# Memory rows, first cached keys and early columns issued singly on the weights' queue; cache consumed at two thirds of the rate; queries one unit sooner

## The chip, the cores and the metric

The kernel runs on one core of one Trainium2 chip. The metric is the device time of one execution in microseconds (us); the median over the runs is compared. The engines are TensorE (PE, with its weight loads shown as PEld), VectorE (DVE), ScalarE (ACT), GpSimd (POOL) and SyncE (SP). SP, ACT and POOL also issue DMAs, each in its own queue.

## The reference, cut to what matters

One decoder layer is computed for two groups at once: a prompt of 256 tokens and 8 single new tokens ("decode" columns). All data is float32.

```
x = LN1(a*x + 0.5*SwiGLU_1(x))
x = LN2(a*x + W_out[RWKV7(x), ConvModule(x)])
x = LN3(a*x + MemCrossAttn(x, mem))        # 4 heads of 512, 256 memory tokens
x = LN4(a*x + 0.5*SwiGLU_2(x))

q = h @ w_mq;  s = q . mk / sqrt(512);  o = softmax(s) . mv;  out = o @ w_mo
prompt: mk, mv = mem @ w_mk, mem @ w_mv          (also returned)
decode: mk, mv = cache_mem_k, cache_mem_v        (8 x 256 x 4 x 512 each)
```

The change touches the stretch from the output projection of the mixer (second line) to that of the cross attention (third line).

## The kernel before, in words

Activations lie transposed: 128 features by 264 columns (256 prompt tokens and 8 decode tokens), 16 such tiles for the 2048 features. Each float32 operand is split into a high and a low float32r part, and a product is three matmuls (`mm3`, L301: lines L303, L304, L305). One such **block** of three matmuls covers 128x128 weights. Weights arrive in chunks of 128x1024 (512 KB, eight blocks) from one long plan: `fetch` (L252) issues them on SP into 3 raw buffers, `prepare` (L270) splits them on ACT (L188) and DVE (L189) into 4 high and 4 low buffers, `chunk` (L292) hands one to `gemm` (L318). So a split of chunk i+3 is emitted when chunk i is taken, and it needs the buffer of chunk i-1, which is free only when TensorE is through with that chunk.

**The order of the work.** The program is written as one driven stream (the matmuls) with side streams. `drive` (L139) adds a planned cost to a planned time `t` after each step of the driven stream (`BLK` = 0.3375 for a block) and then lets every side run that is due; a side's `yield` says how much planned time must pass before its next step. `finish` (L144) runs a side to its end at once, without waiting for planned time. An instruction is placed in its engine's queue by this order, though the scheduler may bring a ready instruction ahead of one that still waits. `with self.behind()` (L174) orders an instruction behind the last weight DMA issued so far, and `issue_after(self.pulse[...])` orders it behind the latest weight split.

**Mixer output projection** (`mixer_out` L1274, `out_proj` L1204). Parts of 512 output columns use all four accumulators (PSUM); DVE adds each accumulator to the residual `y` (L1243). After the second part the function `after` closes the mixer's memory and calls `att_start` (L1373), which calls `mem_reload` (L1321): 16 DMAs on POOL's queue bring back the 16 memory rows (128 KB each), and each row is split by ACT (L1328) and DVE (L1329).

**Memory units** (`mem_kv` L1331). A unit is 256 columns of the prompt's keys or values, 32 blocks. Four units are done earlier, in the LN1 stage; their results are read back from the outputs (`kv_early` L1400: 4 DMAs of 256 KB on SP). `LN2_UNITS` = 3 units run while LN2 is applied (`ln_apply` L411 as a side with a pace of 1.46: three DVE and two ACT instructions for each of 16 rows). Then `finish(*b.sides)` empties what is left of it.

**Attention** (`attention` L1406). Four query GEMMs (one per head, 64 blocks each, planned 21.6), each evicted by ACT (L1419), then the other 9 units (planned 10.8 each). Sides: `att_prompt` (L1448) for the prompt, and `att_decode` (L1489) for the cache. The cache is 64 tiles of 512 KB in 5 buffers, loaded on POOL's queue (L1502): for heads 0 to 3, in the order k0 k1 v0 k2 v1 v2 k3 v3, eight tiles each. A key tile also needs a broadcast query row (`qb`, 256 KB, L1509) and costs two DVE instructions (L1542). A value tile costs ACT L1565, DVE L1566, ACT `vh` (L188), DVE `vl` (L189) and two matmuls (L1571, L1572). Eight key tiles are followed by `dec_softmax` (L1547), eight value tiles by `dec_out` (L1576), which writes the decode columns of the head's output. After each tile the side waits `KV_GAPS` of planned time: 3.0 for a key, 1.5 for a value.

**Attention output projection** (`att_out` L1589, parts in `att_plan` L1358): six parts of 256 output columns over heads 0 to 2 (three chunks each), then six parts over head 3 (one chunk each), then two parts over all heads. Before each block row of head j it asks that the decode side be through with head j:

```
def ready(k):
    while self.decoded < k // 4:
        self.dec.step(self.t)
```

If the side is not that far in planned time, its steps are emitted there and then, ahead of the matmul.

Of the kernel before, what the change touches and what calls it, by code (L numbers as in the profile page):

```python
# [8 lines left out]
F32 = mybir.dt.float32  # L9
F32R = mybir.dt.float32r  # L10
I32 = mybir.dt.int32
AF = mybir.ActivationFunctionType
ALU = mybir.AluOpType
# [5 lines left out]
KD = 16  # L19
TP = 256  # L20
# [33 lines left out]
class Builder:  # L54
# [1266 lines left out]
    def mem_reload(self):  # L1321

        self.mh, self.ml = self.rawtiles()
        for k in range(KD):
            hi, lo = self.mh[k][:, :TP], self.ml[k][:, :TP]
            raw = lo.bitcast(F32)
            self.nc.gpsimd.dma_start(raw, self.mkeep[:, k])
            self.nc.scalar.activation(hi, raw, AF.Copy)  # L1328
            self.nc.vector.tensor_tensor(lo, raw, hi.bitcast(F32), ALU.subtract)  # L1329

    def mem_kv(self, unit, dest):  # L1331

# [40 lines left out]
    def att_start(self, pool):  # L1373
        nc = self.nc
        self.mx = pool
        self.banks(1)
        self.mem_reload()
        eye = self.mt("eye", (128, TB, TB), F32R)
        z = self.mt("eye0", (128, TB * TB))
        nc.vector.memset(z, 0.0)  # L1380
        nc.vector.memset(z[:, 0 : TB * TB : TB + 1], 1.0)
        nc.scalar.activation(eye.rearrange("p a b -> p (a b)"), z, AF.Copy)
        self.eye = eye
        self.kvn = {}
        self.qs = {}
        self.oh = None
# [13 lines left out]
    def kv_early(self, units):  # L1400

        for u in units:
            o, cg, _ = u
            self.nc.sync.dma_start(self.kv_dest(u)(), self.kv_rows(o, cg))

    def attention(self, P, units):  # L1406
        nc = self.nc
# [81 lines left out]
    def att_decode(self):  # L1489

        order = [("k", 0), ("k", 1), ("v", 0), ("k", 2), ("v", 1), ("v", 2), ("k", 3), ("v", 3)]
        items = [(n, h, b) for n, h in order for b in range(TB)]
        keys = [(h, b) for n, h, b in items if n == "k"]
        nc, I = self.nc, self.I
        tiles, qb, pc = [], [], {}

        def load():
            while len(tiles) < len(items) and len(tiles) < self.used + KV_BUFS:
                n, h, b = items[len(tiles)]
                t = self.mt("kv", (128, 2, 512), bufs=KV_BUFS)  # L1500
                src = I["cache_mem_" + n][0, b, :, h].rearrange("(j s) d -> s j d", s=128)
                nc.gpsimd.dma_start(t, src)  # L1502
                tiles.append(t)

        def queries(n):
            while len(qb) < min(n, len(keys)) and keys[len(qb)][0] < len(self.scr):
                h, b = keys[len(qb)]
                t = self.mt("qb", (128, 512), bufs=3)
                nc.gpsimd.dma_start(t, self.scr[h][b : b + 1].to_broadcast([128, 512]))  # L1509
                qb.append(t)  # L1510

        self.used = nk = 0
        for n, h in order:
            while h >= len(self.scr):
                yield 0.6
            if n == "k":
                sc = self.mt("dsc", (128, 2, TB), bufs=2)
                for b in range(TB):
                    queries(nk + 2)
                    load()  # L1520

                    with self.tc.issue_after(self.pulse[1].ins):
                        self.dec_score(tiles[self.used], qb[nk], sc, b)
                    nk += 1
                    self.used += 1
                    yield KV_GAPS[0]
                pc[h] = yield from self.dec_softmax(sc)
            else:
                po = self.held.tile([128, 512], F32, tag="po", name=self.uid("po"))
                for b in range(TB):  # L1530
                    load()
                    with self.tc.issue_after(self.pulse[0].ins):
                        sums = self.dec_value(tiles[self.used], pc[h], po, b)
                    self.used += 1
                    yield KV_GAPS[1]
                    sums()
                yield from self.dec_out(h, po)
            self.decoded = h if n == "v" else self.decoded
# [167 lines left out]
WARM = 8  # L1706
FIRST = 0, 3, 3
LOAD = 7.8
KV_GAPS = 3.0, 1.5
OUT_PARTS = ((0, [0, 1, 2, 3, 8, 9, 10, 11]), (8, []), (12, [12, 13, 14, 15]))  # L1710
FLUSH = 3.5, 1.72
ATT_GAPS = 1.24, 2.0, 3.5, 0.6
VBUFS = 2
LN_PACE = 2.4, 1.46
LN1_UNITS, LN2_UNITS, KV_BUFS = 4, 3, 5


def chained(wait, gen):
    yield wait
    yield from gen  # L1720


def program(tc, I, O):
    with ExitStack() as es:
        b = Builder(tc, I, O, es)
        b.consts()
        b.mark = b.xkeep = b.stats = b.lastfn = b.table = None
        P1 = b.ffn_plan(I["ffn1_w1"][0], I["ffn1_w3"][0], I["ffn1_w2"][0])
        units = b.mem_plan()
        b.plan_add([[u[2]] for u in units[:LN1_UNITS]])  # L1730
        PX = b.mixer_plan()
        PA = b.att_plan(units[LN1_UNITS:])
        P2 = b.ffn_plan(I["ffn2_w1"][0], I["ffn2_w3"][0], I["ffn2_w2"][0])

        with tc.tile_pool(name="mem", bufs=1) as mpool:
            b.place(mpool, GAPS[0])
            with tc.tile_pool(name="ffn1", bufs=1) as pool:
                b.gate_places(pool, 0, GAPS[1])
                b.xs = b.load_x(mpool)

                def ffn1():
                    g = b.ffn(pool, P1)
                    n = 0
                    while True:
                        try:
                            c = next(g)
                        except StopIteration as e:
                            b.L = e.value
                            return
                        n += 1  # L1750
                        if n == 100:
                            b.lnv = b.loaded("lnv", [128, 8 * KD])
                            b.start(b.mixer_consts())
                        if n == 300:
                            b.start(b.mem_rows(mpool))
                        yield c

                b.drive(ffn1())
                b.start(b.ln_apply(b.L, "ln1", 4 * EPS), LN_PACE[0])
                for u in units[:LN1_UNITS]:  # L1760
                    b.drive(b.mem_kv(u, lambda: mpool.tile([128, 2, 256], F32, tag="mo", name=b.uid("mo"), bufs=1)))
                b.finish(*b.sides)
        mix = ExitStack()
        pool = mix.enter_context(tc.tile_pool(name="mix", bufs=1))
        y = b.ytiles()
        b.oa, b.cc = y[:8], y[8:]
        b.drive(b.mixer(pool, PX))

        att = ExitStack()

        def after():
            mix.close()
            b.raw = es.enter_context(tc.tile_pool(name="raw", bufs=1))
            for k in range(KD):
                b.place(b.raw, 128 if k else GAPS[2], (f"rh{k}", T + 2, F32R), (f"rl{k}", T + 2, F32R))
            b.att_start(att.enter_context(tc.tile_pool(name="att", bufs=1)))

        b.drive(b.mixer_out(PX, after))
        b.start(b.ln_apply(b.L, "ln2", EPS), LN_PACE[1])
        rest = units[LN1_UNITS:]  # L1780
        b.kv_early(units[:LN1_UNITS])
        for u in rest[:LN2_UNITS]:
            b.drive(b.mem_kv(u, b.kv_dest(u)))
        b.finish(*b.sides)
        b.drive(b.attention(PA, rest[LN2_UNITS:]))
        b.drive(b.att_out(PA))
        att.close()
        b.banks()
        with tc.tile_pool(name="ffn2", bufs=1) as pool:
            b.gate_places(pool, KD, GAPS[3])  # L1790

            def ffn2():
                b.L = yield from b.ffn(pool, P2, b.L)

            rows = b.start(chained(300.0, b.final_start(pool)))
            states = b.start(chained(80.0, b.rw_states(pool)))
            b.drive(ffn2())
            b.finish(states, rows)
            b.final(b.L, pool)


def build(tc, I, O):
    if MANUAL:
        with tc.manual_schedule():
            program(tc, I, O)
    else:
        program(tc, I, O)
# [66 lines left out]
```

## Time and profile before

| | us |
|---|---|
| median of 3 runs | 2519.65 |
| lowest, highest | 2515.61, 2521.88 |
| profiled execution, its own time | 2526.33 |
| its span in the profile | 2524.6 |
| busy PE, DVE, ACT, POOL | 2470.9, 1582.8, 1195.0, 261.7 |
| mean granted TensorE clock | 0.993 |

The page says what the engines did in 2524.6 us. Matmuls overlap in the pipeline, so a busy share of 98% does not say how fast TensorE went; the count of matmuls in a stretch and the granted clock do. All stretches below are in us from the span's start.

### The profile page before, as it was taken

How to read it: one execution, taken by the hardware profiler on the slowest of the kernel's cores; microseconds unless marked ns; L12 is line 12 of the kernel's file. 1: busy time of each engine (PE TensorE's matmuls, PEld its weight loads, DVE VectorE, ACT ScalarE, POOL GpSimd, SP SyncE). 2: the span in 40 equal slices, each digit the busy share in tenths (PEclk: the TensorE clock that was granted, in tenths of full speed). 3: DMA queues.
4: the chain of work that ended last, by engine and by line, in shares of the span. 5: the costliest groups of instructions: out<-in, count | busy, mean ns of one | idle time of the engine just before them, and what ended most of it. 6: DMA issues, size and time to landing. Idle time of an engine off the chain costs nothing. (4 is left out here: it accounts for less than half of the span.)

```text
span 2524.6 us, 53420 instructions
## 1 busy us (share of the span) xinstructions
PE 2470.9 (98%) x22328; PEld 2417.2 (96%) x22328; DVE 1582.8 (63%) x2545; ACT 1195.0 (47%) x1802; POOL 261.7 (10%) x422
## 2 busy tenths in 40 slices
PE   9999999999999999999989999999999999999998
PEld 9999999999999988988889888989999999999998
DVE  5545444444557599799777566789655545554465
ACT  5444433444446555455646354657444434444443
POOL 1300000000000001000110222220132500000000
PEclk9999999999999999999999999999999999999999
DMA  7656655555557754544476799976677755655554
GB/s 228 188 183 220 203 183 182 183 183 178 179 181 212 221 151 132 149 131 139 128 251 224 262 293 305 322 226 191 195 215 217 237 182 184 183 178 183 176 180 131
DMA packets 452211, 497.89 MB, mean 197 GB/s; under 512 B 22096, under 2 KB 418640, under 8 KB 451968
## 3 DMA queue, kind: packets, MB, share of 16 engines
q1 hardware_dynamic: 417840, 417.09, 54.0%
q0 software_dynamic: 20992, 67.22, 8.4%
q10 hardware_dynamic: 13136, 10.15, 1.2%
q8 instruction: 175, 2.87, 0.5%
q14 instruction: 68, 0.56, 0.1%
HBM read 477.76 MB, written 16.63 MB: 196 GB/s over the span
## 5 line engine op out<-in xcount | busy, mean ns | idle before, releaser
L189 DVE TENSOR_TENSOR wlo<-raw,whi 128x1024 fp32r<-128x1024 f32 (+1 forms) x791 | 961.4, 1216 | 850.6 <-ACT whi L188 847.3
L188 ACT ACTIVATE whi<-raw 128x1024 fp32r<-128x1024 f32 (+1 forms) x791 | 823.0, 1041 | 1035.6 <-PE acc L304 856.6
L303 PE MATMUL acc<-xh,whi 128*128 128x264 f32 x2864 | 828.7, 290 | 15.3 <-DVE y L1243 7.3
L304 PE MATMUL acc<-xl,whi 128*128 128x264 f32 x2864 | 820.2, 287 | 0.6 <-DVE xl L189 0.6
L305 PE MATMUL acc<-xh,wlo 128*128 128x264 f32 x2864 | 816.7, 286 | 0.5 <-DVE wlo L189 0.5
L303 PEld LDWEIGHTS acc<-xh,whi 128*128 128x128 f32 x2864 | 540.3, 189 | 23.8 <-ACT rh L1328 7.5
L304 PEld LDWEIGHTS acc<-xl,whi 128*128 128x128 f32 x2864 | 542.0, 189 | 3.7 <-DVE xl L189 0.8
L305 PEld LDWEIGHTS acc<-xh,wlo 128*128 128x128 f32 x2864 | 541.0, 189 | 2.3 <-DVE wlo L189 1.1
L303 PE MATMUL acc<-rh,whi 128*128 128x264 f32 (+2 forms) x1600 | 456.8, 285 | 0.2 <-ACT lnx L397 0.2
L305 PE MATMUL acc<-rh,wlo 128*128 128x264 f32 (+2 forms) x1600 | 454.5, 284 | 0.0
L304 PE MATMUL acc<-rl,whi 128*128 128x264 f32 (+2 forms) x1600 | 453.4, 283 | 0.0
L304 PE MATMUL acc<-gl,whi 128*128 128x264 f32 x1408 | 400.2, 284 | 0.0
L305 PE MATMUL acc<-gh,wlo 128*128 128x264 f32 x1408 | 400.1, 284 | 0.0
L303 PE MATMUL acc<-gh,whi 128*128 128x264 f32 x1408 | 399.5, 284 | 0.0
L303 PEld LDWEIGHTS acc<-rh,whi 128*128 128x128 f32 x1600 | 300.8, 188 | 2.2 <-ACT lnx L397 0.4
L304 PEld LDWEIGHTS acc<-rl,whi 128*128 128x128 f32 x1600 | 301.7, 189 | 1.2
L305 PEld LDWEIGHTS acc<-rh,wlo 128*128 128x128 f32 x1600 | 300.7, 188 | 0.2
L305 PEld LDWEIGHTS acc<-gh,wlo 128*128 128x128 f32 x1408 | 264.5, 188 | 0.1
L304 PEld LDWEIGHTS acc<-gl,whi 128*128 128x128 f32 x1408 | 264.5, 188 | 0.0
L303 PEld LDWEIGHTS acc<-gh,whi 128*128 128x128 f32 x1408 | 264.3, 188 | 0.1
L1176 DVE SCALAR_TENSOR_TENSOR y<-u,cw,y 128x256 f32<-128x256 f32 x240 | 111.1, 476 | 0.6
L397 ACT ACTIVATE lnx<-acc 128x264 f32<-128x264 f32 x84 | 32.4, 386 | 64.8 <-PE acc L305 64.8
(350 smaller groups left out, 2089.9 us busy)
## 6 DMA issues: line engine op xcount, KB each, us to landing
raw<-in_ffn_w SPq DMA_DIRECT2D x509, 512.0 KB, 3.6
raw<-in_w_in SPq DMA_DIRECT2D x86, 512.0 KB, 3.8
raw<-in_w_mk SPq DMA_DIRECT2D x32, 512.0 KB, 3.4
raw<-in_w_mv SPq DMA_DIRECT2D x32, 512.0 KB, 5.4
raw<-in_w_out SPq DMA_DIRECT2D x32, 512.0 KB, 5.1
kv<-in_cache_mem_k POOLq DMA_DIRECT2D x32, 512.0 KB, 6.2
raw<-in_w_mq SPq DMA_DIRECT2D x32, 512.0 KB, 5.2
kv<-in_cache_mem_v POOLq DMA_DIRECT2D x32, 512.0 KB, 6.1
```

Source lines behind the costliest of these rows:

```text
L188: a = self.nc.scalar.activation(hi, src, AF.Copy)
L189: return a, self.nc.vector.tensor_tensor(lo, src, hi.bitcast(F32), ALU.subtract)
L303: nc.tensor.matmul(out, wh, xh, start=start, stop=False)
L304: nc.tensor.matmul(out, wh, xl, start=False, stop=False)
L305: self.mark = nc.tensor.matmul(out, wl, xh, start=False, stop=stop)
L397: self.lastfn = self.nc.scalar.activation(*args, **kw)
L1176: V.scalar_tensor_tensor(c[:, :TP], u[:, i : i + TP], w(i), c[:, :TP], ALU.mult, ALU.add)
```

## The change

`mem_reload` becomes a side: its 16 DMAs move from POOL's queue to SP's, each behind the last weight DMA, one per step, with the split of a row four steps after its DMA (`MEM_AHEAD` 4, `MEM_PACE` 1.5). A new side `kv_ahead` loads the first five cache tiles on SP's queue in the same manner; it waits `KV_WAIT` = 24.0 of planned time first, then 4.5 after each tile. `kv_early` becomes a side with a gap of 4.5. `KV_GAPS` goes from 3.0, 1.5 to 5.0, 2.5. `LN2_UNITS` goes from 3 to 2, so that the queries come one unit sooner and ten units follow them.

```
     def mem_reload(self):
         self.mh, self.ml = self.rawtiles()
-        for k in range(KD):
-            hi, lo = self.mh[k][:, :TP], self.ml[k][:, :TP]
-            raw = lo.bitcast(F32)
-            self.nc.gpsimd.dma_start(raw, self.mkeep[:, k])
-            self.nc.scalar.activation(hi, raw, AF.Copy)
-            self.nc.vector.tensor_tensor(lo, raw, hi.bitcast(F32), ALU.subtract)
+        for k in range(KD + MEM_AHEAD):
+            if k < KD:
+                with self.behind():
+                    self.nc.sync.dma_start(self.ml[k][:, :TP].bitcast(F32), self.mkeep[:, k])
+            if k >= MEM_AHEAD:
+                hi, lo = self.mh[k - MEM_AHEAD][:, :TP], self.ml[k - MEM_AHEAD][:, :TP]
+                self.split_from(lo.bitcast(F32), hi, lo)
+            yield MEM_PACE
+
+    def kv_ahead(self):
+        yield KV_WAIT
+        for b in range(KV_BUFS):
+            t = self.mt("kv", (128, 2, 512), bufs=KV_BUFS)
+            src = self.I["cache_mem_k"][0, b, :, 0].rearrange("(j s) d -> s j d", s=128)
+            with self.behind():
+                self.nc.sync.dma_start(t, src)
+            self.kvtiles.append(t)
+            yield KV_PACE
...
-        self.mem_reload()
+        self.reload = self.start(self.mem_reload())
+        self.kvtiles = []
...
-            self.nc.sync.dma_start(self.kv_dest(u)(), self.kv_rows(o, cg))
+            with self.behind():
+                self.nc.sync.dma_start(self.kv_dest(u)(), self.kv_rows(o, cg))
+            yield KV_PACE
...
-        tiles, qb, pc = [], [], {}
+        tiles, qb, pc = self.kvtiles, [], {}
...
-KV_GAPS = 3.0, 1.5
+KV_GAPS = 5.0, 2.5
...
-LN1_UNITS, LN2_UNITS, KV_BUFS = 4, 3, 5
+LN1_UNITS, LN2_UNITS, KV_BUFS = 4, 2, 5
+MEM_AHEAD, MEM_PACE, KV_WAIT, KV_PACE = 4, 1.5, 24.0, 4.5
...
-        b.kv_early(units[:LN1_UNITS])
+        b.finish(b.reload)
+        for u in units[:LN1_UNITS]:
+            b.kv_dest(u)()
+        ahead = b.start(b.kv_ahead())
         for u in rest[:LN2_UNITS]:
             b.drive(b.mem_kv(u, b.kv_dest(u)))
-        b.finish(*b.sides)
+        b.finish(ahead, *b.sides)
+        b.start(b.kv_early(units[:LN1_UNITS]))
         b.drive(b.attention(PA, rest[LN2_UNITS:]))
```

## Rows read from the trace of the kernel before

**Rows 1.** The page's first part: busy time of the engines, share of the span, instructions.

```profile
PE 2470.9 (98%) x22328; PEld 2417.2 (96%) x22328; DVE 1582.8 (63%) x2545; ACT 1195.0 (47%) x1802; POOL 261.7 (10%) x422
```

**Rows 2.** Busy time of each engine in chosen stretches: the stretch, its length, busy us and instructions of PE, PEld, DVE, ACT and POOL, the granted clock, the DMA share, GB/s. The first row is undisturbed FFN work. The others are, in order: the reload in the mixer's output projection, the rest of that projection, the three units, the queries, the nine units, the attention's output projection.

```profile
400.00:600.00 200.00, 200.00 (x1650) 200.00 (x1649) 96.69 (x101) 82.44 (x101) 0.00 (x0) 1.00 0.59 182
1255.00:1300.00 45.00, 37.68 (x285) 37.08 (x284) 29.22 (x58) 21.57 (x37) 13.13 (x23) 0.92 0.75 251
1300.00:1332.00 32.00, 32.00 (x265) 31.97 (x265) 27.98 (x56) 15.93 (x26) 0.00 (x0) 1.00 0.56 182
1332.00:1367.00 35.00, 35.00 (x291) 34.70 (x290) 32.00 (x67) 25.32 (x47) 0.00 (x0) 1.00 0.72 226
1367.00:1473.00 106.00, 99.05 (x788) 97.29 (x786) 58.34 (x96) 43.56 (x61) 19.47 (x31) 0.97 0.81 267
1473.00:1626.00 153.00, 144.68 (x1062) 133.98 (x1063) 107.72 (x207) 88.90 (x176) 42.16 (x66) 0.99 0.92 301
1626.00:1736.00 110.00, 105.21 (x818) 102.09 (x818) 90.41 (x179) 57.85 (x93) 23.29 (x38) 0.98 0.77 240
```

**Rows 3.** What TensorE waited for in the stretch 1255 to 1736: us in total, times, longest.

```profile
PE acc L303 <- DVE y L1243: 7.3, 1, 7.3
PE acc L303 <- ACT y L1419: 6.7, 4, 5.2
PE mis L1557 <- DVE p L1446: 4.5, 3, 2.2
PE mis L1481 <- ACT y L1419: 3.7, 1, 3.7
PE po L1571 <- ACT vh L188: 2.3, 2, 1.2
PE mis L349 <- DVE lns L345: 1.9, 1, 1.9
```

**Rows 4.** The timeline at the reload, of ACT, DVE and PE: start, length, engine, line, operation, output and input, count, and the idle time before it with what ended it.

```profile
1269.36 1.32 ACT L1328 ACTIVATE rh<-rl 128x256 fp32r<-128x256 f32 x3 [0.74 <-DMA rl<-mem]
...
1274.60 1.04 ACT L188 ACTIVATE whi<-raw 128x1024 fp32r<-128x1024 f32 x1
...
1275.67 1.23 DVE L189 TENSOR_TENSOR wlo<-raw,whi 128x1024 fp32r<-128x1024 f32 x1 [3.07 <-ACT whi L188]
1276.82 1.44 DVE L1243 TENSOR_TENSOR y<-y,acc 128x264 f32<-128x264 f32 x4
...
1277.38 0.56 PE L303 MATMUL acc<-xh,whi 128*128 128x264 f32 x1 [7.32 <-DVE y L1243]
```

**Rows 5.** What ACT waited for among the queries (1367 to 1473).

```profile
ACT whi L188 <- DMA raw<-in_w_mq: 27.9, 11, 7.9
```

**Rows 6.** The same columns as rows 2, in slices of 20 us.

```profile
1260.00:1280.00 20.00, 12.68 (x95) 12.50 (x94) 13.54 (x28) 10.87 (x22) 13.13 (x23) 0.86 0.91 302
1280.00:1300.00 20.00, 20.00 (x161) 19.97 (x161) 13.50 (x27) 6.80 (x8) 0.00 (x0) 0.97 0.77 264
1400.00:1420.00 20.00, 15.02 (x124) 14.80 (x122) 9.74 (x21) 5.36 (x6) 5.08 (x8) 0.94 0.91 307
1420.00:1440.00 20.00, 19.73 (x146) 19.43 (x147) 13.58 (x24) 7.89 (x11) 5.10 (x8) 0.89 0.82 253
1620.00:1640.00 20.00, 20.00 (x156) 19.58 (x156) 13.53 (x44) 9.89 (x24) 5.11 (x8) 1.00 1.03 356
```

**Rows 7.** DMA issues from 1200 to 1720: transfer, queue, count, KB each, median us to landing.

```profile
kv<-in_cache_mem_k POOLq DMA_DIRECT2D x32, 512.0 KB, 6.2
raw<-in_w_mq SPq DMA_DIRECT2D x32, 512.0 KB, 5.2
...
qb<-scr POOLq DMA_DIRECT2D x32, 256.0 KB, 7.0
...
rl<-mem POOLq DMA_DIRECT2D x16, 128.0 KB, 5.5
```

**Rows 8.** The timeline at the start of the attention's output projection, of DVE (a key tile of head 3) and of PE (the first matmul of the projection).

```profile
1625.99 0.69 DVE L1542 CUSTOM_DVE_ANT_0 kv<-kv,qb 128x512 f32<-128x512 f32 x1
...
1626.31 0.28 PE L303 MATMUL acc<-xh,whi 128*128 128x264 f32 x1
```

**Rows 9.** The instructions on the cache tiles: engine, operation, count, duration in ns (least, median, most), first and last start in us; the last line is of their loads.

```profile
L1565 ACT ACTIVATE kv<-kv,pc x32: 705/709/725, 1487.9 to 1675.2; 128x512 f32<-128x512 f32 x32
L1566 DVE SCALAR_TENSOR_TENSOR kv<-kv,pc x32: 719/745/750, 1488.8 to 1678.2; 128x512 f32<-128x512 f32 x32
L188 ACT ACTIVATE vh<-kv x32: 611/630/634, 1489.6 to 1679.1; 128x512 fp32r<-128x512 f32 x32
L189 DVE TENSOR_TENSOR vl<-kv,vh x32: 672/693/694, 1490.2 to 1680.3; 128x512 fp32r<-128x512 f32 x32
...
DMA to landing us min/median/max: 4.2/6.2/10.3
```

**Rows 10.** The timeline of head 3's softmax and values, of DVE, PE, ACT and POOL: the last key tile, the softmax's first and last steps, the first scaled value tile, two loads, the last value tile, and `dec_out`.

```profile
1651.73 0.68 DVE L1542 CUSTOM_DVE_ANT_0 kv<-kv,qb 128x512 f32<-128x512 f32 x1
...
1655.30 0.41 DVE L1442 TENSOR_REDUCE mx<-mis 8x1 f32<-8x256 f32 x1
...
1662.27 0.28 PE L1557 MATMUL mis<-ident,p 8*128 8x8 f32 x2 [2.25 <-DVE p L1446]
...
1662.81 1.95 ACT L1565 ACTIVATE kv<-kv,pc 128x512 f32<-128x512 f32 x3
...
1666.57 1.57 POOL L1502 DMA_DIRECT2D kv<-in_cache_mem_v  x2 [13.14 <-DVE vl L189]
...
1680.34 0.68 DVE L189 TENSOR_TENSOR vl<-kv,vh 128x512 fp32r<-128x512 f32 x1
...
1682.15 0.41 PE L1584 MATMUL mis<-ident,r 8*128 8x8 f32 x4
```

**Rows 11.** The weight splits from 1200 to 1720: line, engine, operation, count, busy us, mean ns.

```profile
L189 DVE TENSOR_TENSOR wlo<-raw,whi 128x1024 fp32r<-128x1024 f32 x138 | 169.5, 1230 | 108.0 <-ACT whi L188 106.4 <-PE mis L1463 1.2
L188 ACT ACTIVATE whi<-raw 128x1024 fp32r<-128x1024 f32 x139 | 147.1, 1058 | 148.6 <-PE acc L304 63.3 <-DMA raw<-in_w_mq 29.8 <-DMA raw<-in_w_mo 17.9
```

**Rows 12.** The last DVE step of LN2's 16 rows: count, durations in ns, first and last start.

```profile
L424 DVE TENSOR_TENSOR xl<-lnx,xh x16: 422/426/435, 1343.1 to 1372.8; 128x264 fp32r<-128x264 f32 x16
```

## The prediction, made before the changed kernel was run

> **What bounds the kernel now.** I read the page's busy shares first, then the stretches, TensorE's waits, and the timelines. TensorE is busy 98% [rows 1], so the time is its work plus its stalls. Undisturbed, 1650 matmuls take 200 us, 0.121 us each [rows 2], a block of three 0.364 us. The change takes no matmul away; it can only move stalls. Those within its reach lie between 1255 and 1736: idle 45-37.68 = 7.3 us at the reload, 7.0 in the queries, 8.3 in the units, 4.8 in the output projection [rows 2], together 27.4. After an idle stretch the granted clock is under full: 0.92, 0.97, 0.99 and 0.98 in these four [rows 2], which is at most 3.6+3.2+1.5+2.2 = 10.5 us of lost work, less what falls into the idle time itself. So about 35 us is all that this change can win, 1.4%.
>
> **What it removes.** *The reload, 7.3 us.* The chain runs backwards from the matmul at 1277.38: it waits for accumulators that DVE empties at 1276.82, behind a weight split at 1275.67, which waits for ACT's half at 1274.60, which stands in ACT's queue behind the splits of memory rows, each waiting for its DMA [rows 4]. Not the bandwidth but the order of ACT's queue holds TensorE. In the changed kernel a row is split four steps after its DMA. A step of 1.5 falls on the planned grid of 0.675, so it takes 2.03 planned, and 2.03x0.364/0.3375 = 2.2 us; four are 8.7 us, above the 5.5 us that such a DMA needs to land [rows 7]. ACT doesn't block; the 20 steps (44 us) end before the projection does at 1332. What stays is the emptying of four accumulators, 1.44 us [rows 4], and some lateness. I take 7 us as gained with its clock loss, between 3 and 9.
>
> The Trainium skill ("DMA: Bandwidth & Descriptors", section "Issuing engines are not separate DMA queues") says that DMAs from several engines end on the same 16 DMA engines and that another issuer saves only issue time. By that the move from POOL's queue to SP's gives nothing by itself, and the sum below would be 7 us worse. No row shows these rows on SP's queue; I count on the delayed split, not on the queue.
>
> *Queries and units.* ACT waits 27.9 us for query weights [rows 5], and TensorE then for evictions that stand behind those splits in ACT's queue: 6.7 and 3.7 us [rows 3]. The weights are late because too much is asked: a chunk is 524 KB per 24 matmuls, 2.91 us, or 180 GB/s; a key tile with its query row is 786 KB [rows 7] per gap of 3.0, which the grid of 1.35 rounds to 4.05 planned or 4.37 us, another 180. The 360 GB/s stand against at most 356 in any slice [rows 6]. With 5.0 the grid gives 5.4 planned, 5.82 us, 135 GB/s, and 315 in all. That fits, so I take 8 us off the queries (idle and clock) and 6 off the units, where the eviction wait of 3.7 and 1.1 of the 6.7 lie; half of the softmax and value waits [rows 3] stay, as they come from the order in the engines. In the output projection 4 us go: the softmax wait of 2.2 moves into what follows, some clock loss goes. Gains: 7+8+6+4 = 25 us; bounds 34, nearly all that there is, and 12, about half of what I take.
>
> **What it adds.** *The decode side no longer fits.* I add up the planned times, rounded up to the grid (1.35 in the queries, 0.675 after). Both kernels start head 0's keys at 25.7 planned after the first query matmul. Before: a key 4.05, later 3.375, a value 2.025. The output projection starts at 183.6 planned, when head 3's fourth key tile is emitted; v2 ended at 173.5 (asked for at 189.0), v3 ends at 219.4 (asked for at 232.2). The trace agrees: that key tile runs at 1625.99, and the projection starts at 1626.31 [rows 8]. After: a key 5.4, a value 2.7, so 8 keys 43.2 and 8 values 21.6. k0 ends at 71.6, k1 116.8, v0 139.1, k2 184.3. The projection starts at 194.4 with four of v1's eight tiles still to come. At its fifth block row `ready` asks for v1, at the ninth for v2: **eleven value tiles are emitted in two bunches (v1's last three and v2's first, then the rest of v2), ahead of matmuls that need them.** The rest of the schedule shifts: k3's last tile comes at 237.6, head 3 is asked for at 243.0, and **softmax and all eight v3 tiles are emitted there at once.**
>
> *First catch-up.* A value tile takes 0.709+0.630 us of ACT and 0.745+0.693 = 1.44 of DVE, 2.78 in a chain [rows 9]; on an idle machine one comes every 1.44. From the projection's start: the split of the fourth chunk ahead waits until TensorE is through with the first chunk at 8x0.364 = 2.9, and takes 1.06+1.23 [rows 11]; the last three v1 tiles behind it end near 10.5. `dec_out` took 1682.15-1681.02 = 1.1 us to its transposes and then some 1.3 of small splits [rows 10]: 13. TensorE has only the first chunk, and one of the next part if the scheduler brings it forward: idle 7 to 10. The second chunk runs to 16; only then is a buffer free for the next split, behind which six v2 tiles stand: 1.06+1.23+6x1.44+1.34+2.4 = 14.7, to 30.6. One more chunk can be brought forward: idle 12 to 15. Together 19 to 25 us; if the scheduler finds more to bring forward, 14. I take 20.
>
> *Second catch-up.* The softmax took 1662.6-1652.4 = 10.2 us in the old order, amid other work [rows 10]; its own steps add up to about 3. Eight values: 8x1.44+1.34 = 12.9; three of them must first be loaded into buffers that come free 2.8 us after the start, with at least 4.2 us to land [rows 9], which adds 0.5 to 2.5. `dec_out` 2.4. Nothing else can run, since the next six chunks all need head 3. Sum 3+14.4+2.4 = 20 us; from below 17, from above what the old trace shows with TensorE running beside it, 1682.2-1655.3 = 27 [rows 10]. I take 20, nearest to the bare durations, because the weight splits stop when TensorE does.
>
> *Clock after three idle stretches.* The 7.3 us idle left 0.86 and 0.97 in two slices, the 5 us idle 0.94 and 0.89 [rows 6], some 2 us of work beyond the idle time. I add 5, between 3 and 8.
>
> *One unit fewer under LN2.* Its 16 rows end at 1372.8, after the queries began [rows 12]. With 21.6 planned instead of 32.4 before `finish`, some eight rows are emitted in one go: 8x3x0.426 = 10.2 us of DVE. The queries use a row per 1.46 us and find them ready, but the next weight splits stand behind. `kv_ahead` waits 24.0, more than these 21.6, so `finish` also issues its five tiles **together, not singly**: 2.6 MB ahead of the next weights, 7.4 us at 356 GB/s [rows 6]. Seven chunks (20 us) of lead cover most. I add 2, bounds 0 and 8. The `kv_early` DMAs, now in the first query, come before the first key tile: nothing.
>
> **Sum.** Added 20+20+5+2 = 47, removed 25: +22 us. Against the profiled execution's 2526.3 us that is 2548; its time is 6.7 above the median of 2519.65, so against the median I say **2541.5**. All bounds at once give 0 (added 14+17+3+0, removed 34) and +56 (added 25+27+8+8, removed 12).
>
> **Rivals.**
> 1. *The catch-ups are hidden: faster.* Place: the two `ready` calls. If the scheduler orders the forced steps so that they run beside matmuls, or DVE and ACT are through with them early, the gain stands alone: 25-2 = 23 us, 2497; with a part of the stalls up to 2512. It decides from the point where both catch-ups with their clock cost less than 15 us. For it: the old trace has v3's tiles running beside matmuls. Against: there they were emitted 12.8 planned us before they were needed; now at the moment. Chance 0.17.
> 2. *They cancel:* catch-ups of 30 instead of 45 in all, within 7.5 us of no change, 2520. Chance 0.14.
> 3. *The reload gains nothing*, because SP's queue now holds rows and weights in one line and weights come late instead: 22+7 = +29, 2548.5. This is the skill's rule above taken alone. For it: 302 GB/s already in 1260 to 1280 [rows 6]. Against: the wait is one of queue order. Chance 0.10.
> 4. *The forecast*, +8 to +42 otherwise: 0.59.
>
> **How the numbers follow.** About 0.3% (7.6 us) is what a measurement of this kernel can tell from no change. Slower is 0.59+0.10 = 0.69, same 0.14, faster 0.17. For 8 in 10 the range leaves out the faster end of the first rival and the joint upper bounds: 2506 to 2562.
>
> **What the changed profile would show.** Right: no wait of L303 on DVE L1243 over 3 us at the reload; TensorE never idle for more than 2 us at once in the queries; three new idle stretches of 5 to 20 us in the output projection, ended by splits of `dec_out` (L189 or L188 on the decode columns), each followed by a clock under 1; value tiles at intervals near 1.4 us in them. Wrong: if those stretches are missing or under 15 us together, the catch-up was mispriced; if waits for query weights remain near 28 us, the demand was not the cause.

## The result and the profile after

The changed kernel takes **2556.69 us** (median of 4 runs, 2555.01 to 2560.45), the kernel before 2518.9 on the same chip (4 runs): ratio **1.014, 95% interval 1.0125 to 1.0156**. That is +38 us; the forecast was +22 to 2541.5, with 2506 to 2562 as the range. Ratios here and below leave out slow executions; the only ones are two of the 12 of experiment 9, which took 4600.43 and 4810.04 us.

The profiled execution of the changed kernel took 2555.01 us with a span of 2553.3, so the two traces differ by 28.7 us of span. The other 9 us of the 38 lie outside them: the trace of before comes from an execution 7.4 us above its median, that of after from one 1.7 below. I explain the 28.7.

First the stretches of the changed kernel that answer to [rows 2] without its first row: the reload, the rest of that projection, the units (two now), the queries, the other ten units, the attention's output projection (stretch, length, busy us and instructions of PE, PEld, DVE, ACT, POOL, granted clock, DMA share, GB/s).

```profile
1245.00:1290.00 45.00, 44.05 (x380) 42.25 (x380) 27.69 (x51) 18.50 (x24) 1.06 (x2) 1.00 0.41 141
1290.00:1321.00 31.00, 31.00 (x257) 30.96 (x256) 30.51 (x64) 18.39 (x34) 0.00 (x0) 1.00 0.70 231
1321.00:1345.00 24.00, 24.00 (x200) 23.70 (x200) 23.38 (x52) 18.56 (x36) 0.00 (x0) 1.00 0.63 208
1345.00:1459.00 114.00, 100.85 (x782) 98.81 (x782) 61.87 (x102) 48.09 (x72) 15.55 (x25) 0.93 0.82 277
1459.00:1607.00 148.00, 147.85 (x1130) 141.59 (x1129) 95.52 (x183) 77.95 (x149) 32.22 (x52) 1.00 0.87 282
1607.00:1757.00 150.00, 123.81 (x845) 108.80 (x845) 112.43 (x216) 75.20 (x127) 37.64 (x57) 0.87 0.70 229
```

The idle time of TensorE at the reload (1.0 us against 7.3) and in the units (0.2 against 8.3) is gone. In the queries it doubled (13.2 against 7.0), and the output projection went from 110 us with 4.8 idle to 150 us with 26.2 idle at a clock of 0.87.

TensorE's longest waits from 1200 to 1800 say who ended these stretches (total us, times, longest), as in [rows 3]:

```profile
PE po L1587 <- ACT vh L188: 12.2, 6, 3.5
PE acc L303 <- ACT whi L188: 11.0, 2, 9.6
PE mis L1573 <- DVE p L1462: 6.7, 2, 6.5
PE acc L303 <- ACT y L1435: 3.4, 2, 3.0
```

L1573, L1587, L1588 and L1600 are L1557, L1571, L1572 and L1584 of before; L1435 is L1419. Value tiles and a softmax now hold TensorE, one weight split holds it for 9.6 us, and the wait on L1243 of the reload has fallen to 0.9 us, further down the list.

For an account in one unit I use **lost time**: for every two matmuls in succession, the interval between their starts less the median interval of that kind of matmul (line and shape) in the same trace, added up by stage. It holds idle time and slow clock together.

| us | before | after | difference |
|---|---|---|---|
| up to the reload | 71.3 | 67.6 | -3.7 |
| reload and rest of that projection | 9.5 | 2.1 | -7.4 |
| queries | 11.0 | 19.5 | +8.5 |
| units behind the queries | 11.3 | 0.6 | -10.7 |
| attention's output projection | 7.9 | 41.0 | +33.1 |
| FFN 2 | 0.4 | 1.8 | +1.4 |
| from the last matmul to the end | 6.4 | 12.5 | +6.1 |
| sum | 117.8 | 145.1 | +27.3 |

The sum is 1.4 us short of the 28.7; these are not placed. Each column is one execution. The change touches nothing ahead of the reload, and yet that row differs by 3.7 us, and it lies between 65 and 73 in the traces of all kernels here: a few us in a row that adds up many stages can be chance.

**The catch-ups.** The timeline of TensorE in the output projection (start, length, tile, idle time before it and what ended it); these rows are the ends of its idle stretches:

```profile
1618.05 0.39 PE L1587 MATMUL po<-vh,eye 128*8 128x512 f32 x1 [2.20 <-ACT vh L188]
...
1622.88 0.59 PE L1600 MATMUL mis<-ident,r 8*128 8x8 f32 x4 [0.68 <-ACT r L1595]
...
1641.59 0.40 PE L1587 MATMUL po<-vh,eye 128*8 128x512 f32 x1 [3.47 <-ACT vh L188]
...
1645.47 0.81 PE L303 MATMUL acc<-xh,whi 128*128 128x264 f32 x2 [0.27 <-ACT xh L188]
...
1695.50 0.38 PE L1573 MATMUL mis<-ident,p 8*128 8x8 f32 x2 [6.52 <-DVE p L1462]
1698.65 0.59 PE L1587 MATMUL po<-vh,eye 128*8 128x512 f32 x1 [2.77 <-ACT vh L188]
...
1712.20 0.81 PE L303 MATMUL acc<-xh,whi 128*128 128x264 f32 x2 [0.27 <-ACT xh L188]
```

And the clock in slices of 5 us around the third (the columns of [rows 2]):

```profile
1685.00:1690.00 5.00, 3.98 (x34) 3.67 (x32) 3.58 (x6) 1.43 (x3) 0.70 (x1) 1.00 0.92 298
1690.00:1695.00 5.00, 0.00 (x0) 0.00 (x0) 3.50 (x7) 2.40 (x4) 0.00 (x0) 0.85 0.88 288
1695.00:1700.00 5.00, 1.35 (x4) 0.47 (x5) 3.52 (x7) 4.05 (x8) 0.14 (x1) 0.50 0.36 120
...
1710.00:1715.00 5.00, 4.05 (x18) 3.30 (x17) 0.67 (x4) 1.30 (x5) 2.52 (x5) 0.50 0.15 55
1715.00:1720.00 5.00, 5.00 (x34) 5.00 (x34) 2.66 (x5) 2.39 (x5) 4.06 (x7) 0.76 0.46 153
1720.00:1725.00 5.00, 5.00 (x44) 5.00 (x43) 5.00 (x8) 2.41 (x5) 4.12 (x7) 1.00 0.70 206
```

From 1615.9 to 1624.9, 1636.5 to 1645.5 and 1688.8 to 1712.2 no block of the projection runs: 9.0+9.0+23.4 = 41.4 us. Only the small matmuls of the value tiles, the softmax and `dec_out` run there, those of a value tile each ended by a split (`vh` on ACT, `vl` on DVE); a busy PE in these slices is not a working projection. When TensorE comes back, the clock is at 0.50 (the lower level, 1.2 GHz): the slices at 0.50 and 0.76 hold 18 and 34 matmuls, the undisturbed one at 1.00 holds 44.

**The start of the queries.** ACT's timeline, and the one row of SP's that matters:

```profile
1356.10 1.23 ACT L422 ACTIVATE lnx<-y,lnv 128x264 f32<-128x264 f32 x2 [1.37 <-DMA kv<-in_cache_mem_k]
...
1359.34 0.61 ACT L422 ACTIVATE lnx<-y,lnv 128x264 f32<-128x264 f32 x1 [1.39 <-DMA keep<-lnx]
1360.99 0.61 ACT L422 ACTIVATE lnx<-y,lnv 128x264 f32<-128x264 f32 x1 [1.04 <-DMA keep<-lnx]
...
1362.13 2.94 ACT L188 ACTIVATE whi<-raw 128x1024 fp32r<-128x1024 f32 x3
```

```profile
1347.84 3.52 SPq L1340 DMA_DIRECT2D kv<-in_cache_mem_k  x5
```

Three weight splits stand in ACT's queue behind the LN2 rows that `finish` emits at once. Two of these rows wait for a `lnx` buffer, which comes free only when its `keep` write has landed (1.39 and 1.04 us), and all five key tiles (2.6 MB) have been issued at 1347.84 to 1351. TensorE waits 9.6 us for the first of the three splits.

**The end.** The closing DRAINs of POOL and of SP, before and then after (line, engine, operation, count: shortest/median/longest ns, first and last start):

```profile
L1870 POOLq DRAIN  x3: 51/99/5795, 2517.6 to 2524.3; - x3
L1870 SPq DRAIN  x3: 7/7/7, 2523.8 to 2524.1; - x3
```

```profile
L1891 POOLq DRAIN  x3: 51/99/12242, 2540.3 to 2553.0; - x3
L1891 SPq DRAIN  x3: 7/7/7, 2546.2 to 2552.8; - x3
```

POOL's long DRAIN took 5.8 us and takes 12.2. Before, it ended at 2517.6+5.8 = 2523.4, and SP came to its own first DRAIN at 2523.8: the two engines were level. After, it ends at 2552.5, 6.3 us behind SP, and all wait for it. From the last matmul to the end it is 12.5 us instead of 6.4: 6.1 us that no step of the forecast has.

### The profile page after: what moved, and what is told of

Read it like the earlier page. It is cut to its first block, busy times and chain, and to the rows that moved or that the text cites. A ratio compares the mean times of both kernels' runs of the same rounds, so it can differ in the third digit from the quotient of the medians.

```text
span 2553.3 us, 53445 instructions
## 1 busy us (share of the span) xinstructions
PE 2480.2 (97%) x22328; PEld 2420.0 (95%) x22328; DVE 1581.7 (62%) x2545; ACT 1197.4 (47%) x1802; POOL 251.7 (10%) x401
## 4 chain that ended last, share of the span: by engine, by line
PE 85%; DVE 5%; DMA 4%; issue 3%; ACT 2%; POOL 0%; SPq 0%; POOLq 0%; ACTq 0%; DVEq 0%
PE acc L303 27%; PE acc L304 27%; PE acc L305 27%; DVE wlo L189 2%; DMA raw<-in_ffn_w 1%; ACT whi L188 1%; DMA raw<-in_w_mq 1%; DMA kv<-in_cache_mem_v 1%; DVE y L1176 1%; PE mis L1473 1%; DMA raw<-in_w_mo 0%; PE mis L1488 0%; DVE G L890 0%; PE mis L850 0%; PE mis L843 0%
## 5 line engine op out<-in xcount | busy, mean ns | idle before, releaser
L303 PE MATMUL acc<-xh,whi 128*128 128x264 f32 x2864 | 829.9, 291 | 18.0 <-ACT whi L188 11.8
L303 PEld LDWEIGHTS acc<-xh,whi 128*128 128x128 f32 x2864 | 541.8, 190 | 26.1 <-ACT whi L188 12.6
L303 PE MATMUL acc<-rh,whi 128*128 128x264 f32 (+2 forms) x1600 | 455.1, 284 | 0.2 <-ACT lnx L397 0.2
L303 PE MATMUL acc<-gh,whi 128*128 128x264 f32 x1408 | 399.6, 284 | 0.1
L303 PEld LDWEIGHTS acc<-rh,whi 128*128 128x128 f32 x1600 | 301.1, 188 | 1.0 <-ACT lnx L397 0.4
L303 PEld LDWEIGHTS acc<-gh,whi 128*128 128x128 f32 x1408 | 264.3, 188 | 0.4 <-ACT lnx L397 0.3
```

The source lines that it names most:

```text
L303: nc.tensor.matmul(out, wh, xh, start=start, stop=False)
```

## The experiments

Ratios are to the kernel before on the same chip, with their 95% intervals.

**1. The changed kernel with the old gaps.**

```
-KV_GAPS = 5.0, 2.5
+KV_GAPS = 3.0, 1.5
```

> The changed kernel with the old gaps (3.0, 1.5). If the decode side that no longer fits is what costs, the idle stretches in the attention's output projection go (33 us of lost TensorE time there against 8 before), the units get back some 5 to 10 us of stalls, and the time is 2526 to 2535 us against 2557. If the queue of the rows or the start of the queries is the main cost, it stays above 2545.

Measured 2527.98 us, 1.0016 (1.0003 to 1.0028). The catch-ups are gone: 5.9 us lost in the output projection. What is left of the change is no gain either. What TensorE still waits for from 1200 to 1800 is led by the split at the start of the queries:

```profile
PE acc L303 <- ACT whi L188: 9.1, 2, 8.5
PE acc L303 <- ACT y L1435: 5.5, 3, 3.9
PE po L1587 <- ACT vh L188: 3.9, 2, 2.1
```

**2. The kernel before with the new gaps alone.**

```
-KV_GAPS = 3.0, 1.5
+KV_GAPS = 5.0, 2.5
```

> The kernel before with the new gaps (5.0, 2.5) alone: 27 steps are then forced in planned time, since the projection is asked for 10.8 earlier than in the changed kernel. If the forced steps are the cost: 33 to 45 us added in the output projection, 15 to 20 removed in queries and units, 2535 to 2548 us. If a slower rate costs nothing by itself: 2500 to 2512 us, as the DMA demand falls.

Measured 2554.57 us, 1.0119 (1.0097 to 1.0140), above the 2535 to 2548 that were expected: one line carries nearly the whole loss. In the output projection 46.5 us are lost; the waits are those of the changed kernel, and that of the reload is still there.

```profile
PE po L1571 <- ACT vh L188: 13.6, 7, 4.2
PE mis L1557 <- DVE p L1446: 10.2, 3, 7.1
PE acc L303 <- DVE y L1243: 8.2, 2, 7.6
```

Taken out, the gaps give 0.0124 back; put in alone, they cost 0.0119: some 30 us either way. The catch-up is shown.

**3, 4, 8, 11. The start of the queries.** Four edits of the changed kernel: `LN2_UNITS` 2 to 3 (experiment 3), `KV_WAIT` 24.0 to 0.0, so that the key tiles come singly (4), `LN_PACE[1]` 1.46 to 1.2, so that by planned time three LN2 rows instead of eight are left for `finish` (8), and 4 with 8 (11).

> The changed kernel with three units before the queries. The stall of 9.6 us and its low clock at the start of the queries (about 14 us in all): if the LN2 rows emitted at once cause it (ACT's queue holds weight splits behind rows that wait for a free buffer), it goes nearly whole, though four more steps are forced later (+3 to 6): 2543 to 2550 us. If the five cache tiles in one go cause it, three of them still come at once, half of it stays: 2550 to 2558 us.

> The changed kernel with no wait before the first cached keys, so that all five come singly during the two units. If the five tiles in one go cause the stall at the start of the queries (about 14 us), it goes: 2541 to 2546 us. If the LN2 rows emitted at once cause it, most stays: 2551 to 2557 us. If both together are needed, it goes as well, so that this run and the one with three units both gain.

> The changed kernel with LN2's rows at a pace of 1.2 instead of 1.46, so that three rows instead of eight are emitted at once before the queries; the five cache tiles still come together. If the rows hold ACT's queue: the stall of 9.6 us at the start of the queries shrinks below 4, 8 to 12 us under the changed kernel. If the five tiles alone do it: it stays above 7.

> The changed kernel with both suspects at the start of the queries removed at once: LN2's rows at a pace of 1.2 and no wait before the five tiles, still two units and gaps of 5.0 and 2.5. Each alone left 18 to 19 us of lost time in the queries. If either of the two is enough to hold ACT's queue, now the loss falls to about 10 us and the time to 2546 to 2550; if something else holds it (two units alone), it stays near 18 and 2553 to 2557.

| | after | 3: three units | 4: tiles singly | 8: three rows left | 11: both |
|---|---|---|---|---|---|
| longest wait of L303 for a split, us | 9.6 | none | 6.4 | 3.7 | none |
| lost in the queries, us | 19.5 | 13.2 | 18.1 | 19.3 | 15.1 |
| of it in the first 96 of their 256 blocks, us | 13.7 | 5.9 | 9.7 | 12.4 | 8.1 |
| median, us | 2556.69 | 2558.12 | 2553.08 | 2557.69 | 2555.02 |
| ratio | 1.0140 | 1.0130 | 1.0115 | 1.0147 | 1.0122 |

Rows in a bunch and tiles in a bunch both lengthen the wait: with either eased a part of it stays, with both (11) or with a third unit, which gives them time (3), it is gone. The lost time does not go with it. In 11 the first 96 blocks still lose 8.1 us, where the kernel before loses 0.5, and the time, 2555.02, is in the range that was named for "something else holds it (two units alone)". With three units, tiles singly and gaps of 4.0 and 2.0 (experiment 10, further down) these blocks lose 2.4 us. So the third unit gives more back than easing the two bunches does; what it gives beyond spacing them is not taken apart (in 11 three rows still come at once). Some time also comes back as waits for query evictions (L1435, in 3 for 4.4 us at most, in 11 for 3.4). The intervals of the four ratios overlap with that of the changed kernel (each some 0.3% wide), so in the total time none of this is resolved, and the gains that were expected for 3, 4 and 8 if their suspect was the cause did not come; what is said here is read from the waits and the lost time.

**5, 6. The reload alone, in the kernel before.** The 16 rows become a side with the split four steps behind its DMA, as in the change; everything else is old. In 5 the rows are on SP's queue, each behind the last weight DMA; in 6 they are on POOL's, without that order.

```
+        for k in range(KD + MEM_AHEAD):
+            if k < KD:
+                with self.behind():                        # 5 alone
+                    self.nc.sync.dma_start(...mkeep[:, k])  # 6: self.nc.gpsimd
+            if k >= MEM_AHEAD:
+                self.split_from(...)
+            yield MEM_PACE
```

> The kernel before with the new reload alone (rows on SP's queue, each behind weights, split four steps later). If ACT's queue order caused the 7.3 us stall: that stall is under 2 us, some 8 us of lost TensorE time go. If the drain of POOL at the very end (5.8 us before, 12.2 us in the changed kernel, whose POOL queue issues 21 DMAs fewer) follows from rows leaving POOL's queue, it takes 6 us back: about 2517 to 2520 us against 2519 to 2524; if that drain has to do with the five cache tiles, it stays at 6 and the time is 2511 to 2515. If the queue itself mattered (rows and weights in one line), no gain at the reload.

> The same delayed split, but the rows stay on POOL's queue. If only the order of the splits matters: the reload's stall goes just as with SP, the final drain stays at 5.8 us, and the time is 6 to 9 us under the kernel before. If the weights' queue matters (rows behind weights and not beside them), the stall stays, and so does the time.

Measured 2523.76 us, 0.9998 (0.9988 to 1.0009), and 2525.27, 1.0019 (1.0009 to 1.0028). The stall at the reload stays: TensorE waits for L1243 9.1 us in 5 and 8.3 in 6. ACT's timeline in 5, then what SP and POOL issued:

```profile
1273.05 1.06 ACT L188 ACTIVATE whi<-raw 128x1024 fp32r<-128x1024 f32 x1 [11.14 <-DMA raw<-in_w_out]
```

```profile
1257.21 1.91 SPq L1406 DMA_DIRECT2D n<-out  x4
1261.38 14.38 SPq L266 DMA_DIRECT2D raw<-in_w_out  x4
```

```profile
1257.73 0.71 POOL L1504 DMA_DIRECT2D kv<-in_cache_mem_k  x1 [28.31 <-ACT xh L188]
...
1259.53 1.43 POOL L1504 DMA_DIRECT2D kv<-in_cache_mem_k  x2
1261.52 1.42 POOL L1504 DMA_DIRECT2D kv<-in_cache_mem_k  x2 [0.55 <-issue]
```

In 5 ACT no longer waits for memory rows; it waits 11.1 us for weights. With the rows out of POOL's queue the scheduler brings the five key tiles forward, to 1257 to 1263 (before, they came at 1274.71 and later). The four columns (L1406, from 1257.21) stand where they stood: at 1260.52 before, in a stretch that began 3 us later. Together these are 3.7 MB, issued just ahead of the next weights and beside them. A new wait has taken the place of the old.

In 6 the old wait has stayed. What ACT waits for from 1255 to 1300, and the tiles on POOL's queue:

```profile
ACT rh L188 <- DMA rl<-mem: 8.7, 9, 3.9
```

```profile
1274.10 3.55 POOL L1503 DMA_DIRECT2D kv<-in_cache_mem_k  x5
```

On POOL's queue, with nothing that orders them behind weights, the 16 rows are issued from 1259.58 to 1273.47, much as before (1261.00 to 1274.18), and the tiles come after them. ACT reaches the splits before their rows have landed, and weight splits stand behind. So 6 does not show what a delayed split alone is worth: in it the splits still wait for their rows.

**7. Gaps that fit.** Experiment 6 with `KV_GAPS` 4.0, 2.0. By the forecast's sum of planned times v3 then ends at 231.5, just before it is asked for at 232.2.

> As the run before, and gaps of 4.0 and 2.0: by planned time the last value tile then ends at 231.5, head 3 is asked for at 232.2, so nothing is forced. If the forced steps, not the slower rate, cost: no idle stretch over 3 us in the output projection beyond what the kernel before has, the units' stalls shrink by some 5 us, 8 to 14 us under the kernel before. If a slower rate costs in itself: slower than the run before it.

Measured 2520.89 us, 0.9998 (0.9989 to 1.0007), against 1.0019 in 6: 2.3 us lost in the units instead of 11.9, and no catch-up (8.5 us lost in the output projection, 7.9 before). Of the 8 to 14 us under the kernel before that were expected, the time shows nothing.

**9. The other half of the reload.** The changed kernel with the old reload (rows on POOL's queue, split at once), tiles and columns singly behind weights, three units, `KV_WAIT` 0, gaps 4.0 and 2.0.

```
-        for k in range(KD + MEM_AHEAD): ...     # the side
+        for k in range(KD): ...                 # as in the kernel before
```

> The other half of the first stretch: the old reload (rows together on POOL's queue, split at once), but the early columns and the first cache tiles singly behind weights; three units, no wait before the tiles, gaps of 4.0 and 2.0. The new reload alone left the stall at the reload, with weights waiting 11 us behind the five tiles and four columns. If either burst is enough to hold TensorE there, the stall stays at 3 to 7 us here too; if the tiles and columns alone made it, it falls under 2. The final drain of POOL (267 DMAs on its queue): 4 to 6 us if it goes with the count as from 272 to 256, 12 if it goes with tiles on SP's queue. In all 6 to 14 us under the kernel before.

Measured ratio 0.9982 (0.9968 to 0.9996), some 4.5 us under the kernel before where 6 to 14 were expected. The stall of the old order is there, though no burst of tiles or columns is. In 9, and then the wait on that stretch in experiment 10, which is 9 with the new reload:

```profile
PE acc L303 <- ACT rh L1328: 6.2, 1, 6.2
```

```profile
PE acc L303 <- DVE y L1243: 1.2, 1, 1.2
```

**10, 12. The best of both.** 10 is the changed kernel with `LN2_UNITS` 3, `KV_WAIT` 0.0 and `KV_GAPS` 4.0, 2.0. 12 is 10 with LN2's 16 `keep` writes on POOL's queue:

```
-            nc.scalar.dma_start(keep, x)
+            (nc.gpsimd if name == "ln2" else nc.scalar).dma_start(keep, x)
```

> The changed kernel with its three flaws mended as the runs point to them: gaps of 4.0 and 2.0 that fit, three units under LN2, no wait before the first tiles. Against the kernel before: 7 to 8 us less lost at the reload, 8 to 10 in the units, some 2 in the queries, nothing in the output projection, 6 more in the final drain of POOL: 8 to 14 us faster. If the drain is not on the path, 14 to 20.

> The fitted kernel with single columns (e10) and one edit: the 16 keep writes of the second layer norm are issued by POOL instead of ACT, so that POOL issues 267 DMAs and not 251. Theory A, the drain at POOL's end goes with what POOL's own queue has issued (272: 5.8 us, 267: 4.8, 256: 4.4, but 251: 12.2 to 12.6) and ends the program: it falls from 12.4 us to about 5, and the time is 5 to 8 us under e10's, about 2514, ratio 0.995 to 0.997 to the kernel before. Theory B, the drain goes with which tiles and columns SP's queue carries: it stays at 12 us and the time at e10's, 0.998 to 1.000. By either, ACT's queue has 16 issues fewer at the second layer norm, worth 0 to 2 us at the start of the queries.

Measured: 10 takes 2521.27 us, 0.9990 (0.9979 to 1.0002); 12 takes **2517.49 us, 0.9971 (0.9957 to 0.9986)**, the lowest ratio here, though its interval overlaps with that of 9. Of the 8 to 14 us that were expected of 10, its interval leaves some 5 at most. The stages of 7 and 10 did gain in their traces, but the trace of before lies 7.4 us above its kernel's median and theirs 2.7 and 3.2 us below; a sum of stages from one execution each is not a difference of medians. The closing DRAIN, in 9, 10 and 12:

```profile
L1888 POOLq DRAIN  x3: 51/99/4817, 2508.7 to 2514.7; - x3
```

```profile
L1891 POOLq DRAIN  x3: 51/112/12412, 2503.1 to 2516.1; - x3
```

```profile
L1891 POOLq DRAIN  x3: 51/112/4816, 2511.5 to 2517.8; - x3
```

16 more DMAs on POOL's own queue make its DRAIN 7.6 us shorter, with tiles and columns on SP's queue as before: theory B falls. In 12 they come from ACT's queue and in 9 from SP's, with the same 4.8 us. How much of it reaches the time is not shown: the ratios of 10 and 12 differ by 0.0019, 5 us, with intervals that overlap, and on different chips; in the traces the stretch from the last matmul to the end is 6.7 us shorter in 12, but its span is 2518.0 us against 2516.3, as queries, units and FFN 2 lost more in that execution. 9 and 10, on one chip, differ by the reload: 7.0 us less lost there in 10, 6.9 more at the end, and ratios that agree within their intervals.

## Why the prediction was right in sign and short in size

**The catch-ups (+20, +20, +5 for the clock, -4 elsewhere in the projection: +41): right.** They took 9.0+9.0 us (forecast 7 to 10 and 12 to 15, so the second was shorter) and 23.4 (forecast 20, from above 27). In the third the softmax alone held TensorE for 6.5 us, between the bare 3 and the 10.2 of [rows 10], and the values came about one per 1.6 us instead of 1.44. At the lower clock, 0.22 instead of 0.121 us per matmul, the three returns lost some 6 us. The stage grew by 40 us (149.9 against 109.3): 33 are lost time, and the rest is work of 13 value tiles (21 against 8) and two `dec_out` that used to run in the units. The first rival, hidden catch-ups, had said that the scheduler finds other work: TensorE ran out of it each time.

**The reload (-7): the size right, the reason half of it.** 7.4 us came back. But the step said that the order of ACT's queue holds TensorE, and the wait had two sufficient causes, one behind the other. The order is one (9: rows split at once, 6.2 us of stall). Bring the rows into order alone and the tiles, which no longer stand behind them in POOL's queue, come early, and ACT waits for weights instead (5: 9.1 us of stall). With both out of the way the stall is 1.2 us (10). Which of tiles and columns delays the weights in 5 is not taken apart. So in the kernel before, this reload alone gains nothing, and the forecast priced the second part, the columns and tiles moved, at nothing: that 7 came out is in part luck. The forecast counted on the delayed split and not on the queue; 6 shows that the delay needs more than the four steps, since on POOL's queue and without the order behind weights 8.3 us of stall stay. The Trainium skill ("DMA: Bandwidth & Descriptors", section "Issuing engines are not separate DMA queues") says that another issuing engine saves issue time alone. With rows on SP's queue (5) as on POOL's (6) the stall stays, which agrees with it, though what holds ACT differs (weights in 5, rows in 6). Yet the forecast drew from it that the reload might gain nothing in the change, and that rival is out.

**The start of the queries (+2, bounds 0 and 8): the term that failed.** Instead of -8+2 = -6 us the queries lost 8.5 more. The lower demand did its part: with the slow gaps alone (2) they lose 7.9 us against 11.0. But ACT's wait for query weights fell only from 27.9 [rows 5] to 22.2 us (19.6 in 2), not far from the 28 that the forecast had named as a sign that demand was not the cause. And its sign that TensorE is never idle for over 2 us in the queries failed. Of the 19.5 us lost, 13.7 are in the first 96 blocks, with the stall of 9.6 us and the low clock after it (0.83 from 1340 to 1380). I had priced the tiles as a transfer of 7.4 us with 20 us of lead and the rows as DVE work, each by itself. What I missed is that they meet in ACT's queue: rows wait for buffers whose `keep` writes have not landed, with the tiles in flight, and three weight splits stand behind the rows. With tiles and rows spaced (11) the wait is gone, but 8.1 of the 13.7 us stay, and with three units 5.9 (3) or 2.4 (10): what the missing unit costs beside the two bunches stays open.

**The units (-6): more than forecast.** 10.7 us of lost time, and the value tiles that left. With gaps 4.0 and 2.0, where less is asked for too, most of it is had without a catch-up (7: 2.3 us lost against 11.9). In the sum this hides part of what the queries lost, which is luck again.

**The end (0): missed.** 6 us, by POOL's DRAIN. Nothing in the trace of before says that its 5.8 us could change.

**Against the median.** In traces I had 2548, it was 2555.0. The other half of the miss is that I took the 6.7 us by which the profiled execution lay above its median off the forecast; the next one lay below its own.

## What to carry to other kernels

- A side stream that is slowed has a length and a deadline. Add up its planned steps, rounded as the planner rounds them, up to where the result is asked for; 4.0 and 2.0 end 0.7 of planned time early, 5.0 and 2.5 cost 30 us.
- A call that empties a stream turns "one by one" into a bunch; look at what its instructions wait for, and what stands behind them on their engine.
- A wait with two sufficient causes shows no gain when one is taken away. Before a part is called worthless, look whether the wait's releaser has changed (5), or whether the edit did what it was meant to (6).
- A wait that is gone is not yet time that is won: 11 ended the wait and kept most of the loss.

## What the runs showed of the hardware that I had not expected

The length of POOL's closing DRAIN depends on what POOL's own DMA queue has issued, not in proportion. With 272 DMAs on it 5.6 to 5.8 us (before, 2, 6, 7), with 267 4.8 (9, 12), with 256 4.4 (5), with 251 12.2 to 12.4 (after, 1, 3, 4, 8, 10, 11). Experiment 12 shows that DMAs added to that queue shorten it; why it jumps between 251 and 256 stays open. Only the long one ends the program: with 251 DMAs it is 12.4 to 12.6 us from the last matmul to the end, and with 256 to 272 between 5.7 and 6.8, not in the order of the DRAINs: 6.7 in 5, where POOL's is the shortest and SP comes to its own 2.0 us after it has ended.
